# A hybrid decoder block: a shrinking lead of first products in the up-projection, and the weight sums of the down-projection spread over three stages

## The chip, the cores and the metric

The kernel runs on one core of one Trainium2 chip. The metric is the device time of one execution in microseconds (us). TensorE is called PE, VectorE DVE, ScalarE ACT, GpSimd POOL, and SyncE, which issues the transfers, SP.

## The reference, cut to what matters

One layer of a decoder block for 1024 tokens of width 1024, in float32. Two token mixers are projected, gated and merged, and a gated MLP follows:

```
y_a = o_a @ w_nsa_branch;  y_b = o_r @ w_ret_branch
x = x + (gate_a * y_a + gate_b * y_b) @ w_mix_out
h = rms_norm(x, norm_ffn_w)
u = causal_dwconv(h @ w_ffn_up, ffn_conv_w, ffn_conv_b)      # 1024 -> 2 x 2816, width 3
u_gate, u_val = split(u, 2)
x = x + (silu(u_gate) * u_val) @ w_ffn_down                  # 2816 -> 1024
return rms_norm(x, norm_final_w)
```

## The kernel before, in words

Each float32 operand of a product is held as a high and a low part, and a product is three passes on PE: high by high, low by high, high by low (`mm3`, line 283). A split is two instructions: ACT writes the high part `wh` (line 175, `split`), and DVE or POOL subtracts it from the source to get the low part `wl` (line 176).

**Up** is done by 2x2 blocks in Winograd's form, with seven products in place of eight. A step `f` (of 22) makes one tile of 128 gate and one of 128 value columns, 7 products of 12 matmuls (128x512) each, 84 in all. Two of them, "11" and "21", need no sums: `start_up` multiplies a11 by block B11, copies the bank to SBUF (ACT, `p1`), and a12 by B21 is added to the same bank. Five need sums: s2·t2, s3·t3, s1·t1, then a22·t4 and s4·B22, where t1 to t4 are sums of h's blocks (made once, split by `sums`) and s1 to s4 are sums of the step's weights, made by DVE a step ahead (`other_weights`, lines 1214 to 1220). a22·t4 is added to the bank `q` of s3·t3, so its first matmul has to wait until DVE has read that bank for `u3` (line 1244). The step's end is DVE's `cg[:, 1]` (line 1255); then follow the convolution, silu and multiplication (lines 1230 to 1259), and the store of the result, `act`.

The raw weights come as 512 KB tiles by `raw_up`: `v` (the pair a21, a22) and `g` (a11, a12), through the two buffers of `wraw`. SP issues in its program order, and a transfer into a buffer waits for the last reader of the tile that was there. Before `up`'s first step, `LEAD` = 5 pairs of the products "11" and "21" are computed ahead, in the place that is called the lead here; h's last transposed blocks (`piece`) and their sums stand between them.

For down, the sums of its weights (11 groups, `t_sums`: four loads, four DVE instructions, four stores of 256 KB each) are made earlier and stored: six in the branch-a stage (the product with w_nsa_branch, line 1012, which also holds transposes), five in the mix stage (the product with w_mix_out). The w_ret_branch stage stands between the two.

The order on each engine is mostly made by a scheduler from the order of emission, which acts as priority, with waits on semaphores. PE's order in the lead and in the mix stage's second half is the order of the code (`manual_schedule`).

Of the kernel before, what the change touches and what calls it, by code (L numbers as in the profile page):

```python
# [10 lines left out]
F32 = mybir.dt.float32  # L11
# [7 lines left out]
P = 128  # L19
# [144 lines left out]
def hybrid_block(ctx: ExitStack, tc: tile.TileContext, a, c, out):  # L164
# [839 lines left out]
    for ch in range(2):  # L1004
        nx = Weights(w_a, 0, 4, [(512, 512)]) if ch == 0 else Weights(w_b, 0, KT, [(0, 512)])
        for i in range(4):
            m = gated(ch * 4 + i)
            ps = ps2.tile([P, S], F32, name="mm2")
            for half in range(2):
                mm3(ps[:, half * 512:half * 512 + 512], lambda part, kt: gw.at(part, kt, i * P, P),  # L1010
                    lambda part, kt: oaT[part][kt][:, half * 4:half * 4 + 4, :].rearrange("p t q -> p (t q)"), 4)
            nc.vector.tensor_mul(m, ps, m)
            ma.append(m)
            if len(t_left) > 5:
                x, y = ([q[:, 0:512], q[:, 512:S]] for q in
                        (mp.tile([P, S], F32, name="tq", tag="gb", bufs=3) for _ in range(2)))
                t_sums(t_left.pop(0), x, y)
            transposed_split(ps1, o_r[ch * 4 + i], *orT, ch * 4 + i)
        gw = nx
    with ort:  # L1020
        craw = wraw.tile([P, 2, 512], F32, name="wr").rearrange("p a b -> p (a b)")
        for i in range(4):
            src = a["ffn_conv_b"][0] if i == 3 else a["ffn_conv_w"][0, i]
            nc.sync.dma_start(craw[:2 * FT, i * P:(i + 1) * P], src.rearrange("(f p) -> f p", p=P))
        pc = ps1.tile([P, 4, P], F32, name="tp")
        for i in range(4):
            nc.tensor.transpose(pc[:, i, :2 * FT], craw[:2 * FT, i * P:(i + 1) * P], ident[:2 * FT, :2 * FT])
        nc.vector.tensor_copy(cw, pc[:, :, :2 * FT])
        for ch in range(2):
            nx = Weights(w_b, 0, KT, [(512, 512)]) if ch == 0 else Weights(w_mix, 0, KT, [(0, 512)])  # L1030
            for i in range(4):
                j = ch * 4 + i
                m = gated(KT + j)
                ps = ps2.tile([P, S], F32, name="mm2")
                mm3t(ps, gw, i * P, orT, KT)
                nc.vector.tensor_mul(m, ps, m)
                nc.vector.tensor_add(m, m, ma[j])
                mhj = big2.tile([P, S], F32R, name="mh", tag="big2")
                mlj = big.tile([P, S], F32R, name="ml", tag="big")
                split(mhj, mlj, m)  # L1040
                mh.append(mhj)
                ml.append(mlj)
            gw = nx
    ms.close()
    pss_.close()
# [32 lines left out]
    def piece(t, h):  # L1078

        at = slice((t % 4) * P, (t % 4) * P + P)  # L1080
        got = []
        for kh in range(2):
            pt = psX.tile([P, 4, P], F32, name="f")
            for i in range(4):
                nc.tensor.transpose(pt[:, i, :], h[kh][:, i * P:(i + 1) * P], ident)
            full = mx.tile([P, 4, P], F32, name="pc", bufs=16)
            nc.scalar.activation(full, pt, AF.Copy)
            if t < 4 or kh:
                k = ("21" if kh else "11") if t < 4 else "22"
                nc.scalar.activation(bh[k][:, :, at], pt, AF.Copy)  # L1090
                nc.vector.tensor_tensor(bl[k][:, :, at], pt, f32(bh[k][:, :, at]), OP.subtract)
            got.append(full)
        low[t] = got
        if t < 4:
            return
        (b11, b21), (b12, b22) = low[t - 4], low[t]
        side = nc.vector if t == NT - 1 else nc.gpsimd
        nc.vector.tensor_tensor(b11, b12, b11, OP.subtract)
        side.tensor_tensor(b12, b22, b12, OP.subtract)
        nc.vector.tensor_tensor(b22, b22, b11, OP.subtract)  # L1100
        side.tensor_tensor(b21, b21, b22, OP.subtract)

    waiting = []

# [16 lines left out]
    pair = []  # L1121
    for t in range(NT):
        residual(t, 0)
        if t in (1, 3, 5, 6, 7) and len(t_left):
            four = [mx.tile([P, 512], F32, name="tq", tag="pc", bufs=16) for _ in range(4)]
            t_sums(t_left.pop(0), four[:2], four[2:])
        if not pair:
            pair = [bank() for _ in range(2 if t in (0, NT - 2) else 1)]
            for k in range(0, KT, 2):
                for i, ps in enumerate(pair):  # L1130
                    mo(ps, t + i, k, k + 2)
        ps = pair.pop(0)
        nc.vector.tensor_add(x1[t][0], ps, x1[t][0])
# [38 lines left out]
    def first_weights(f):  # L1172

        g = raw_up(f, 0)
        p = parts2(g, nc.gpsimd)
        return {k: [x[:, i] for x in p] for i, k in enumerate(("a11", "a12"))}, g

    def prod(ps, w, k, first=True, last=True):
        mm3(ps, lambda part, kt: w[part][:, kt * P:(kt + 1) * P], lambda part, kt: (bh, bl)[part][k][:, kt, :], 4,
# [2 lines left out]
    def start_up(w):  # L1182
        x = bank()
        prod(x, w["a11"], "11")
        p1 = c2()
        nc.scalar.activation(p1, x, AF.Copy)  # L1186
        return x, p1

    sums([4, 5])
    uw, begun = {}, {}  # L1190
    for f in range(LEAD):
        uw[f], _ = first_weights(f)
        begun[f] = start_up(uw[f])
        if f in (0, 2):
            t = waiting[0][0]
            piece(*waiting.pop(0))
            sums([t])
        prod(begun[f][0], uw[f]["a12"], "21", False, True)
    pe_order.close()
    mix.close()  # L1200

# [5 lines left out]

    act_d = [dram.tile([P, 2, 512], F32, name=f"act{f}") for f in range(FT)]

    def other_weights(f, w, g=None):  # L1210
        v = raw_up(f, 1)
        g = g or raw_up(f, 0)
        s = c4()
        nc.vector.tensor_add(s[:, 0], v[:, 0], v[:, 1])
        nc.vector.tensor_sub(s[:, 1], s[:, 0], g[:, 0])
# [16 lines left out]
        nc.vector.scalar_tensor_tensor(y[:, 2:], src[:, :S - 2], cw[:, 0, f:f + 1], y[:, 2:], op0=OP.mult, op1=OP.add)  # L1232
        return y

    def up(f, w, begun=None):
        x, p1 = begun or start_up(w)
        y = bank()
        prod(y, w["s2"], "t2")
        u2 = c2()
# [4 lines left out]
        nc.vector.tensor_add(u3, q, u2)  # L1244
        z = bank()
        prod(z, w["s1"], "t1")
        cg, cv = c4(), c4()
        nc.vector.tensor_add(cv[:, 1], z, u3)
        if not begun:
            prod(x, w["a12"], "21", False, True)  # L1250
        nc.scalar.activation(cg[:, 0], x, AF.Copy)
        prod(q, w["a22"], "t4", False, True)
        nc.vector.tensor_add(cv[:, 0], q, u2)
        prod(z, w["s4"], "22", False, True)
# [5 lines left out]
        yg = yg.rearrange("p (a b) -> p a b", b=512)  # L1260
        nc.sync.dma_start(act_d[f], yg)

    def weights(f):
        if f in uw:
            return other_weights(f, uw.pop(f))
        return other_weights(f, *first_weights(f))

    nx = weights(0)
    for f in range(FT):
        w, nx = nx, weights(f + 1) if f + 1 < FT else None  # L1270
        up(f, w, begun.pop(f, None))
    tp.close()
    ups.close()


    STEPS = [(j, min(2, HT - j)) for j in range(0, HT, 2)]
    NS = len(STEPS)
    keep = ctx.enter_context(tc.tile_pool(name="keep", bufs=1, side="right", reuse_waits="tile"))
    sparts = ctx.enter_context(tc.tile_pool(name="sparts", bufs=3, side="right", reuse_waits="tile"))
    raws = ctx.enter_context(tc.tile_pool(name="raws", bufs=3, side="right", reuse_waits="tile"))  # L1280
    xp = ctx.enter_context(tc.tile_pool(name="xp", bufs=1, reuse_waits="tile"))
    kp2 = ctx.enter_context(tc.tile_pool(name="keep2", bufs=1, reuse_waits="tile"))
    W = {"b11": (0, 0), "b21": (1, 0), "b22": (1, 1)}
    A = {"a11": (0, 0), "a12": (1, 0), "a21": (0, 1), "a22": (1, 1)}
    kept = {}

    def fetch_a(k, i, dst):
        (kh, sh), (j, n) = A[k], STEPS[i]
        for x in range(n):
            nc.sync.dma_start(dst[:, x], act_d[kh * HT + j + x][:, sh])  # L1290
        return dst

    def held(k, i):
        if (k, i) not in kept:
# [29 lines left out]
            "a22": lambda i: held("a22", i)}  # L1324

    def prepared(sk, tk, i):
        j, n = STEPS[i]
        t = wraw.tile([P, 2, 512], F32, name="wr")
        if tk in W:
            kh, nh = W[tk]  # L1330
            r0 = (kh * HT + j) * P
            src = w_dn[r0:r0 + n * P, nh * 512:nh * 512 + 512].rearrange("(k p) n -> p k n", p=P)
        else:
            src = t_d[int(tk[1]) - 1][j:j + n].rearrange("k p n -> p k n")
        nc.sync.dma_start(t[:, :n], src)
        s = S_OF[sk](i)
        got = []
        for x, pool, names in ((s, sparts, ("sh", "sl")), (t, wpool, ("wh", "wl"))):
            p = [pool.tile([P, 2, 512], F32R, name=k) for k in names]
            split(p[0][:, :n], p[1][:, :n], x[:, :n])  # L1340
            got.append(p)
        return got
# [68 lines left out]
                ("s3", "t3", "y", True, done_7, True), ("s4", "b22", "z", True, done_3, True),  # L1411
                ("a22", "t4", "y", True, done_4, False)]
    units = [(i, j) for i in range(7) for j in range(NS)]
    ready = {}
    banks = {}
    later = []
    AHEAD = 2
# [1 line left out]
    for at, (i, j) in enumerate(units):  # L1419
        for x in units[at:at + AHEAD + 1]:  # L1420
            if x not in ready:
                ready[x] = prepared(*PRODUCTS[x[0]][:2], x[1])
        if i == 1:
            held("a21", j)
            held("a22", j)
        if i == 1 and j:
# [61 lines left out]
```

## Time and profile before

| | |
|---|---|
| median of 3 runs (lowest, highest) | 1812.72 us (1809.72, 1813.13) |
| profiled execution, its own time | 1812.5 us |
| its span | 1810.7 us |
| PE busy | 97% of the span |
| mean granted clock of PE | 0.99 |
| stretch from the end of step 0 to up's end | 1184.87 to 1585.24 us |

The median is over whole executions; the span is the part of the profiled one that the trace covers, and times in the trace count from its start. A granted clock of 1.00 is PE at 2.4 GHz.

### The profile page before, as it was taken

The numbers are of one execution on the slowest core, as the hardware profiler recorded it, in microseconds if no ns is written. First come the engines' busy times: TensorE is split into PE (matmuls) and PEld (weight loads), VectorE is DVE, ScalarE is ACT, GpSimd is POOL, SyncE is SP. The second block draws the span as 40 slices with busy tenths as digits, with TensorE's granted clock in tenths as the row PEclk, the third lists the DMA queues.
The fourth block names the chain that finished last, engine by engine and source line by source line (L and its number), as shares of the span: only waits on it lengthen the run. The fifth ranks groups of instructions, "written<-read, shape, count | busy, mean of one in ns | idle before, by whom it ended". The sixth has DMA issues, their size and how long they took to land.

```text
span 1810.7 us, 22500 instructions
## 1 busy us (share of the span) xinstructions
PE 1750.6 (97%) x8331; PEld 1434.6 (79%) x8331; DVE 1186.5 (66%) x2337; ACT 804.2 (44%) x1464; POOL 126.6 (7%) x78
## 2 busy tenths in 40 slices
PE   7999999999999999999989999789999999999998
PEld 6987888888788888888868877667888888878886
DVE  7445877777875554455644446767767777678666
ACT  6334666666662344136332215434444444343344
POOL 0000020110100000000000002301121211000000
PEclk9999999999999999999989999899999999999999
DMA  6121010110202111101682383322322322395353
GB/s 227 55 82 53 19 56 32 36 59 18 71 24 94 47 37 57 47 1 47 231 270 93 93 300 137 99 70 70 104 71 82 93 70 87 108 354 189 94 163 111
DMA packets 87418, 178.88 MB, mean 99 GB/s; under 512 B 8508, under 2 KB 18316, under 8 KB 87308
## 3 DMA queue, kind: packets, MB, share of 16 engines
q1 hardware_dynamic: 87308, 177.44, 30.2%
q8 instruction: 65, 1.06, 0.2%
q14 instruction: 45, 0.37, 0.1%
HBM read 137.57 MB, written 39.85 MB: 98 GB/s over the span
## 4 chain that ended last, share of the span: by engine, by line
PE 60%; DVE 5%; DMA 4%; ACT 2%; issue 2%; SPq 1%; POOL 1%; DVEq 0%; POOLq 0%; ACTq 0%
PE f L283 33%; PE mm L283 19%; PE fill L772 2%; DMA tq<-in_w_ffn_down 2%; PE po L826 1%; PE pv L718 1%; PE pt L706 1%; PE sc L610 1%; DMA wr<-in_w_ffn_up 1%; PE pst L826 1%; DMA wr<-in_w_mix_out 0%; ACT wh L209 0%; PE pss L871 0%; DVE c L1231 0%; DVE c L1232 0%
## 5 line engine op out<-in xcount | busy, mean ns | idle before, releaser
L283 PE MATMUL mm<-wh,hh 128*128 128x512 f32 (+1 forms) x576 | 224.0, 389 | 0.5 <-ACT hh L175 0.5
L283 PE MATMUL mm<-wh,hl 128*128 128x512 f32 (+1 forms) x576 | 219.8, 382 | 0.0
L283 PE MATMUL mm<-wl,hh 128*128 128x512 f32 (+1 forms) x576 | 219.8, 382 | 0.0
L209 ACT ACTIVATE wh<-wr 128x1024 fp32r<-128x1024 f32 (+1 forms) x72 | 74.6, 1037 | 167.0 <-PE mm L283 83.2
L713 DVE TENSOR_TENSOR pl<-pt,ph 128x512 fp32r<-128x512 f32 (+1 forms) x148 | 100.6, 686 | 41.8 <-ACT ph L710 41.2
L283 PEld LDWEIGHTS mm<-wh,hl 128*128 128x128 f32 x576 | 108.8, 189 | 20.6 <-DVE hl L176 0.3
L283 PEld LDWEIGHTS mm<-wh,hh 128*128 128x128 f32 x576 | 108.8, 189 | 20.2 <-ACT hh L175 0.9
L283 PE MATMUL f<-wh,sh 128*128 128x512 f32 x308 | 121.6, 395 | 3.3 <-ACT sh L175 3.3
L710 ACT ACTIVATE ph<-pt 128x512 fp32r<-128x512 f32 (+1 forms) x148 | 87.7, 594 | 82.8 <-PE pt L706 74.5
L283 PEld LDWEIGHTS mm<-wl,hh 128*128 128x128 f32 x576 | 108.9, 189 | 19.5 <-DVE wl L215 0.5
L283 PE MATMUL f<-wl,sh 128*128 128x512 f32 x308 | 121.5, 395 | 0.0
L283 PE MATMUL f<-wh,sl 128*128 128x512 f32 x308 | 120.7, 395 | 0.0
L283 PE MATMUL f<-bh,wh 128*128 128x512 f32 x264 | 105.0, 398 | 11.9 <-ACT c L1186 11.9
L176 POOL TENSOR_TENSOR wl<-wr,wh 128x1024 fp32r<-128x1024 f32 x22 | 53.6, 2438 | 898.3 <-ACT wh L175 883.4
L283 PE MATMUL f<-bht,wh 128*128 128x512 f32 x264 | 104.8, 397 | 8.3 <-ACT wh L175 8.3
L772 PE MATMUL fill<-hh,wh 128*128 128x512 f32 x256 | 104.5, 408 | 3.0 <-ACT sg L784 2.0
L283 PE MATMUL f<-bht,wl 128*128 128x512 f32 x264 | 105.0, 398 | 2.2 <-DVE wl L176 2.2
L628 ACT ACTIVATE big<-big,st 128x640 f32<-128x640 f32 (+7 forms) x128 | 93.4, 730 | 28.1 <-DVE st L624 27.3
L215 DVE TENSOR_TENSOR wl<-wr,wh 128x1024 fp32r<-128x1024 f32 (+1 forms) x60 | 71.5, 1193 | 51.2 <-ACT wh L209 50.2
L283 PE MATMUL f<-blt,wh 128*128 128x512 f32 x264 | 104.4, 395 | 0.0
L283 PE MATMUL f<-bl,wh 128*128 128x512 f32 x264 | 104.1, 394 | 0.0
L283 PE MATMUL f<-bh,wl 128*128 128x512 f32 x264 | 103.4, 393 | 0.0
(282 smaller groups left out, 4127.6 us busy)
## 6 DMA issues: line engine op xcount, KB each, us to landing
wr<-in_w_ffn_up SPq DMA_DIRECT2D x49, 512.0 KB, 4.7
wr<-in_w_in SPq DMA_DIRECT2D x40, 512.0 KB, 3.7
tq<-in_w_ffn_down SPq DMA_DIRECT2D x44, 256.0 KB, 4.7
t<-tq SPq DMA_DIRECT2D x44, 256.0 KB, 3.0
act<-c SPq DMA_DIRECT2D x22, 512.0 KB, 2.8
wr<-t SPq DMA_DIRECT2D x20, 512.0 KB, 3.5
a<-act SPq DMA_DIRECT2D x33, 256.0 KB, 6.0
gate<-sg SPq DMA_DIRECT2D x32, 256.0 KB, 2.0
```

Of the source, the lines that this page charges most:

```text
L176: (engine or nc.vector).tensor_tensor(lo, src, f32(hi), OP.subtract)
L209: nc.scalar.activation(hi[:, :, :self.n], self.raw[len(self.hi)], AF.Copy)
L215: self.engine.tensor_tensor(lo[:, :, :self.n], self.raw[j], f32(self.hi[j][:, :, :self.n]), OP.subtract)
L283: nc.tensor.matmul(ps, stat(sp, kt), mov(mp, kt), start=(first and n == 0), stop=(last and n == 3 * nk - 1), skip_group_check=more)
L610: nc.tensor.matmul(out[:, c0:c0 + n], q[:, h, :], mov, start=(q is box["h"]), stop=(q is box["l"]))
L628: nc.scalar.activation(probs[b][h], probs[b][h], AF.Exp, scale=-1.0, bias=stat["nm", b][:, h:h + 1], accum_out=stat["w", b][:, h:h + 1])
L706: nc.tensor.transpose(bx["pt"][:rows, h, :], probs[h][:, k * P:k * P + rows], ident)
L710: nc.scalar.activation(bx["h"][:rows], bx["pt"][:rows], AF.Copy)
L713: nc.vector.tensor_tensor(bx["l"][:rows], bx["pt"][:rows], f32(bx["h"][:rows]), OP.subtract)
L718: nc.tensor.matmul(acc["pv"], v, bx[part][:rows].rearrange("p h q -> p (h q)"), start=start, stop=stop)
L772: nc.tensor.matmul(fx["ps"], w.at(sp, kt, i * P, P), hT[mp][:, kt, half * 512:half * 512 + 512], start=(n == 0), stop=(n == 3 * KT - 1))
L826: nc.tensor.matmul(ps[:, h, :], stat[sp][:, h, :], mov[mp][:, h, :], start=(first and n == 0), stop=(last and n == 2))
```

## The change

In `up`, each step first starts the pairs of later steps: the lead is 5 pairs at the start and shrinks to one (`max(1, LEAD - f // 4)` ahead). Their products "11" and "21" are emitted before a22·t4 of the current step. The weights of the pairs are now fetched apart from those of the sums: three raw tiles in a step where before there were two (from step 5 on, `g` was fetched once for both uses). `sums` is emitted after the five leads instead of between them. `piece` makes all its four sums on DVE. The 11 groups of `t_sums` are spread 4, 3 and 4 over the branch-a stage, the w_ret_branch stage and the mix stage. The last step of up also prepares the first unit of down. PE's work is the same in number and kind.

```diff
-            if len(t_left) > 5:
+            if (ch * 4 + i) % 2 == 0:
                 x, y = ([q[:, 0:512], q[:, 512:S]] for q in
                         (mp.tile([P, S], F32, name="tq", tag="gb", bufs=3) for _ in range(2)))
                 t_sums(t_left.pop(0), x, y)
...
+                if j in (2, 4, 6):
+                    x, y = ([q[:, 0:512], q[:, 512:S]] for q in
+                            (mp.tile([P, S], F32, name="tq", tag=f"ma{j - k}") for k in (2, 1)))
+                    t_sums(t_left.pop(0), x, y)
...
-        side = nc.vector if t == NT - 1 else nc.gpsimd
         nc.vector.tensor_tensor(b11, b12, b11, OP.subtract)
-        side.tensor_tensor(b12, b22, b12, OP.subtract)
+        nc.vector.tensor_tensor(b12, b22, b12, OP.subtract)
         nc.vector.tensor_tensor(b22, b22, b11, OP.subtract)
-        side.tensor_tensor(b21, b21, b22, OP.subtract)
+        nc.vector.tensor_tensor(b21, b21, b22, OP.subtract)
...
-        if t in (1, 3, 5, 6, 7) and len(t_left):
+        if t % 2 and t_left:
...
-    sums([4, 5])
-    uw, begun = {}, {}
+    fw, begun = {}, {}
     for f in range(LEAD):
-        uw[f], _ = first_weights(f)
-        begun[f] = start_up(uw[f])
+        fw[f] = first_weights(f)
+        begun[f] = start_up(fw[f])
         if f in (0, 2):
-            t = waiting[0][0]
             piece(*waiting.pop(0))
-            sums([t])
-        prod(begun[f][0], uw[f]["a12"], "21", False, True)
+        prod(begun[f][0], fw[f]["a12"], "21", False, True)
+    sums([4, 5, 6])
+    sums([7])
...
-    def other_weights(f, w, g=None):
-        v = raw_up(f, 1)
-        g = g or raw_up(f, 0)
+    def other_weights(f):
+        w = {}
+        v, g = raw_up(f, 1), raw_up(f, 0)
...
-    def up(f, w, begun=None):
-        x, p1 = begun or start_up(w)
+    def up(f, w, x, p1, ahead):
+
+        cg, cv = c4(), c4()
+        nc.scalar.activation(cg[:, 0], x, AF.Copy)
         y = bank()
         prod(y, w["s2"], "t2")
...
-        if not begun:
-            prod(x, w["a12"], "21", False, True)
-        nc.scalar.activation(cg[:, 0], x, AF.Copy)
+        for k in ahead:
+            begun[k] = start_up(fw[k])
+            prod(begun[k][0], fw.pop(k)["a12"], "21", False, True)
         prod(q, w["a22"], "t4", False, True)
...
+    at = LEAD
     for f in range(FT):
-        w, nx = nx, weights(f + 1) if f + 1 < FT else None
-        up(f, w, begun.pop(f, None))
+        w, nx = nx, other_weights(f + 1) if f + 1 < FT else None
+        upto = min(FT, f + 1 + max(1, LEAD - f // 4))
+        for k in range(at, upto):
+            fw[k] = first_weights(k)
+        if f == FT - 1:
+            s = fetch_a("a11", 0, wraw.tile([P, 2, 512], F32, name="wr"))
+            ready[0, 0] = [parts2(s, nc.vector), parts2(fetch_t("b11", 0), nc.vector)]
+        up(f, w, *begun.pop(f), range(at, upto))
+        at = max(at, upto)
```

What this makes of the order on the engines is seen at three places.

PE, in the middle of up, where a22·t4 begins. `bh11` and `bl11` are the parts of B11, the names with t1 and t4 those of the sums; `a22h`, `a22l`, `wh` and `wl` are weights. Before, step 8:

```order
L283 MATMUL f_11800<-bh11_9529,wl_11640 128x512 [waits Pool_49]
L283 MATMUL f_11800<-bh11_9529,wh_11639 128x512
L283 MATMUL f_11800<-bl11_9532,wh_11639 128x512
L283 MATMUL f_11800<-bh11_9529,wl_11640 128x512
L283 MATMUL f_11800<-bh11_9529,wh_11639 128x512
L283 MATMUL f_11800<-bl11_9532,wh_11639 128x512
L283 MATMUL f_11800<-bh11_9529,wl_11640 128x512
L283 MATMUL f_11693<-bht4_10404,a22h_11522 128x512 [waits DVE_49]
L283 MATMUL f_11693<-blt4_10405,a22h_11522 128x512
```

Now, step 2:

```order
L283 MATMUL f_11029<-bht1_10400,wl_10837 128x512
L283 MATMUL f_11014<-bht4_10402,a22h_10847 128x512 [waits DVE_49]
L283 MATMUL f_11014<-blt4_10403,a22h_10847 128x512
L283 MATMUL f_11014<-bht4_10402,a22l_10848 128x512
L283 MATMUL f_11014<-bht4_10402,a22h_10847 128x512
L283 MATMUL f_11014<-blt4_10403,a22h_10847 128x512
L283 MATMUL f_11043<-bh11_9543,wh_10992 128x512 [waits Activation_49]
L283 MATMUL f_11043<-bl11_9546,wh_10992 128x512
L283 MATMUL f_11043<-bh11_9543,wl_10993 128x512 [waits Pool_49]
```

Before, the product with B11 of a later step stood ahead of a22·t4, after t2, t3, t1 and the step's own product "21". Now a22·t4 follows t1 directly: five matmuls, then B11 of a pair of the lead (12 matmuls), four of a22·t4, B21 of the pair (12), three of a22·t4, and s4·B22 (12). Steps 3, 6, 7, 10, 11, 14, 15, 18, 19 and 20 read the same, and steps 5, 9, 13 and 17 nearly so (a22·t4 cut into 6, 2 and 4). Step 1 has B11 ahead of a22·t4. Steps 4, 8, 12, 16 and 21 start no pair; there a22·t4 and B22 follow t1 (and 11 matmuls of the next step's t2).

SP, the raw weights of a step and the store of a result. Before:

```order
L1169 DMA wr_11010<-in_w_ffn_up 128x1024 [waits DMAHW7_49,DVE_49,Pool_49]
L1169 DMA wr_11012<-in_w_ffn_up 128x1024 [waits DMAHW0_49,DVE_49]
L1261 DMA act2_10650<-c4_10999 128x1024 [waits DVE_49]
```

Now; `wr_10990` becomes the `wh_10992` and `wl_10993` of the rows on PE, and `wr_11107` and `wr_11109` are v and g of the sums of a later step:

```order
L1172 DMA wr_10990<-in_w_ffn_up 128x1024 [waits DMAHW1_49,DVE_49,Pool_49]
L1172 DMA wr_11107<-in_w_ffn_up 128x1024 [waits DMAHW3_49,DVE_49]
L1172 DMA wr_11109<-in_w_ffn_up 128x1024 [waits DMAHW5_49,Pool_49]
L1264 DMA act2_10648<-c4_11096 128x1024 [waits DVE_49]
```

There are three tiles in place of two through the same two buffers. The first takes the buffer of a v, whose last reader on DVE is line 1221 (1219 before), the second that of a g, the third that of the first, which POOL's split has read.

SP, in the branch-a stage, around the load of the fifth gate tile (`ma<-gate_1647`). Before:

```order
L202 DMA wr<-in_w_ret_branch 128x2x512
L989 DMA tq<-in_w_ffn_down 128x512
L990 DMA tq<-in_w_ffn_down 128x512
L202 DMA wr<-in_w_ret_branch 128x2x512
L978 DMA ma_8796<-gate_1647 128x1024
L997 DMA t_8525<-tq 128x512
```

Now:

```order
L997 DMA t_8526<-tq 128x512
L202 DMA wr<-in_w_ret_branch 128x2x512
L978 DMA ma_8768<-gate_1647 128x1024
L202 DMA wr<-in_w_ret_branch 128x2x512
L989 DMA tq<-in_w_ffn_down 128x512
L990 DMA tq<-in_w_ffn_down 128x512
```

In the whole queue, 16 loads of down's weights and 13 stores of sums stood ahead of this gate tile before, and 8 loads and 8 stores now.

## Rows read from the trace of the kernel before

**Rows 1.** The page: share of busy time, and the granted clock in 40 slices.

```profile
PE 1750.6 (97%) x8331; PEld 1434.6 (79%) x8331; DVE 1186.5 (66%) x2337; ACT 804.2 (44%) x1464; POOL 126.6 (7%) x78
PEclk9999999999999999999989999899999999999999
```

**Rows 2.** Windows: stretch, length, busy us of each engine, PE's clock, DMA share, GB/s.

```profile
860.00:934.00 74.00, 66.57 (x307) 53.48 (x305) 46.03 (x59) 26.03 (x34) 0.00 (x0) 0.95 0.75 252
934.00:1022.00 88.00, 87.57 (x364) 70.43 (x365) 34.92 (x32) 23.01 (x22) 0.00 (x0) 0.94 0.30 101
1132.00:1140.00 8.00, 3.71 (x9) 2.96 (x10) 7.88 (x17) 5.87 (x12) 1.28 (x1) 0.57 0.23 80
1166.00:1237.00 71.00, 59.39 (x240) 45.56 (x239) 49.67 (x58) 24.81 (x27) 5.16 (x4) 0.96 0.26 88
1237.00:1585.00 348.00, 348.00 (x1506) 282.71 (x1504) 252.47 (x288) 148.76 (x161) 62.07 (x34) 1.00 0.27 86
```

**Rows 3.** Timeline of PE: first matmuls after its waits (start, length, and idle time before).

```profile
934.43 0.82 PE L283 MATMUL mm<-orT,wh 128*128 128x512 f32 x2 [2.61 <-DVE ma L1012]
1078.68 0.49 PE L283 MATMUL f<-wh,mh 128*128 128x512 f32 x1 [2.15 <-ACT wh L209]
1136.29 0.80 PE L283 MATMUL f<-bh,wh 128*128 128x512 f32 x1 [7.04 <-ACT c L1186]
1146.69 0.80 PE L283 MATMUL f<-bh,wh 128*128 128x512 f32 x1 [3.07 <-ACT c L1186]
1213.25 0.50 PE L283 MATMUL f<-bht,wh 128*128 128x512 f32 x1 [3.59 <-ACT wh L175]
1588.50 0.50 PE L283 MATMUL f<-wh,sh 128*128 128x512 f32 x1 [3.26 <-ACT sh L175]
```

**Rows 4.** Timeline of SP in steady up: three stores of results, and weight fetches.

```profile
1382.22 0.33 SPq L1261 DMA_DIRECT2D act<-c  x1
1401.15 0.33 SPq L1261 DMA_DIRECT2D act<-c  x1
1401.79 2.03 SPq L1169 DMA_DIRECT2D wr<-in_w_ffn_up  x2
1420.07 0.33 SPq L1261 DMA_DIRECT2D act<-c  x1
```

**Rows 5.** Timeline of DVE, PE, ACT and POOL in one step of steady up.

```profile
1392.45 0.69 DVE L1255 TENSOR_TENSOR c<-f,c 128x512 f32<-128x512 f32 x1 [2.04 <-PE f L283]
1401.04 0.69 DVE L1219 TENSOR_TENSOR c<-wr 128x512 f32<-128x512 f32 x1
1404.17 0.69 DVE L1244 TENSOR_TENSOR c<-f,c 128x512 f32<-128x512 f32 x1
1405.65 0.40 PE L283 MATMUL f<-bht,a22h 128*128 128x512 f32 x1
1406.83 1.06 ACT L175 ACTIVATE wh<-wr 128x1024 fp32r<-128x1024 f32 x1 [0.84 <-DMA wr<-in_w_ffn_up]
1407.97 2.41 POOL L176 TENSOR_TENSOR wl<-wr,wh 128x1024 fp32r<-128x1024 f32 x1 [15.61 <-ACT wh L175]
```

**Rows 6.** The page's transfers: line, count, size, median us from issue to landing.

```profile
wr<-in_w_ffn_up SPq DMA_DIRECT2D x49, 512.0 KB, 4.7
```

**Rows 7.** Timeline of PE: the last of the 24 matmuls after each lead wait.

```profile
1143.23 0.39 PE L283 MATMUL f<-bh,wl 128*128 128x512 f32 x1
1153.51 0.40 PE L283 MATMUL f<-bh,wl 128*128 128x512 f32 x1
```

**Rows 8.** Timeline in the lead: a sum on DVE alone, and beside POOL.

```profile
1127.48 0.68 DVE L1098 TENSOR_TENSOR pc<-pc 128x512 f32<-128x512 f32 x1
1138.72 2.40 POOL L176 TENSOR_TENSOR wl<-wr,wh 128x1024 fp32r<-128x1024 f32 x1 [7.07 <-ACT wh L175]
1138.92 2.74 DVE L1098 TENSOR_TENSOR pc<-pc 128x512 f32<-128x512 f32 x1
```

**Rows 9.** Timeline of DVE: the end of step 0.

```profile
1184.87 0.69 DVE L1255 TENSOR_TENSOR c<-f,c 128x512 f32<-128x512 f32 x1 [2.04 <-PE f L283]
```

More of the change, by code (lines that the diff above doesn't have):

```diff
@@ L1175, in first_weights @@
         p = parts2(g, nc.gpsimd)
-        return {k: [x[:, i] for x in p] for i, k in enumerate(("a11", "a12"))}, g
+        return {k: [x[:, i] for x in p] for i, k in enumerate(("a11", "a12"))}
     def prod(ps, w, k, first=True, last=True):
@@ L1246, in up @@
         prod(z, w["s1"], "t1")
-        cg, cv = c4(), c4()
         nc.vector.tensor_add(cv[:, 1], z, u3)
-        if not begun:
-            prod(x, w["a12"], "21", False, True)
-        nc.scalar.activation(cg[:, 0], x, AF.Copy)
+        for k in ahead:
+            begun[k] = start_up(fw[k])
+            prod(begun[k][0], fw.pop(k)["a12"], "21", False, True)
         prod(q, w["a22"], "t4", False, True)
@@ L1261, in up, with fetch_a, fetch_t @@
         nc.sync.dma_start(act_d[f], yg)
[L1263 to L1268, printed above, removed]
-    for f in range(FT):
-        w, nx = nx, weights(f + 1) if f + 1 < FT else None
-        up(f, w, begun.pop(f, None))
+    STEPS = [(j, min(2, HT - j)) for j in range(0, HT, 2)]
+    NS = len(STEPS)
+    A = {"a11": (0, 0), "a12": (1, 0), "a21": (0, 1), "a22": (1, 1)}
+    W = {"b11": (0, 0), "b21": (1, 0), "b22": (1, 1)}
+    def fetch_a(k, i, dst):
+        (kh, sh), (j, n) = A[k], STEPS[i]
+        for x in range(n):
+            nc.sync.dma_start(dst[:, x], act_d[kh * HT + j + x][:, sh])
+        return dst
+    def fetch_t(k, i):
+        j, n = STEPS[i]
+        t = wraw.tile([P, 2, 512], F32, name="wr")
+        if k in W:
+            kh, nh = W[k]
+            r0 = (kh * HT + j) * P
+            src = w_dn[r0:r0 + n * P, nh * 512:nh * 512 + 512].rearrange("(k p) n -> p k n", p=P)
+        else:
+            src = t_d[int(k[1]) - 1][j:j + n].rearrange("k p n -> p k n")
+        nc.sync.dma_start(t[:, :n], src)
+        return t
+    ready = {}
+    nx = other_weights(0)
+    at = LEAD
+    for f in range(FT):
+        w, nx = nx, other_weights(f + 1) if f + 1 < FT else None
[7 more added lines that the diff above has]
+        at = max(at, upto)
     tp.close()
     ups.close()
-    STEPS = [(j, min(2, HT - j)) for j in range(0, HT, 2)]
-    NS = len(STEPS)
     keep = ctx.enter_context(tc.tile_pool(name="keep", bufs=1, side="right", reuse_waits="tile"))
@@ L1282, in hybrid_block @@
     kp2 = ctx.enter_context(tc.tile_pool(name="keep2", bufs=1, reuse_waits="tile"))
-    W = {"b11": (0, 0), "b21": (1, 0), "b22": (1, 1)}
-    A = {"a11": (0, 0), "a12": (1, 0), "a21": (0, 1), "a22": (1, 1)}
     kept = {}
[L1287 to L1291, printed above, removed]
     def held(k, i):
@@ L1326, in prepared @@
     def prepared(sk, tk, i):
[L1327 to L1335, printed above, removed]
+        n = STEPS[i][1]
+        t = fetch_t(tk, i)
         s = S_OF[sk](i)
@@ L1413, in hybrid_block @@
     units = [(i, j) for i in range(7) for j in range(NS)]
-    ready = {}
     banks = {}
@@ L1423, in hybrid_block @@
         if i == 1:
+            held("a11", j)
             held("a21", j)
```

## The prediction

> **What bounds the kernel now.** I read the page's shares first: PE is busy 97% of the span at nearly full clock everywhere [rows 1]. So time can be won only from PE's waits and the stretches of low clock, and lost wherever PE has to wait anew. The windows then show where that is [rows 2]. In steady up, from 1237 to 1585, PE is busy 348.00 of 348.00 us at clock 1.00: nothing is to be won there. The branch-a stage (860 to 934) leaves 74.00 - 66.57 = 7.4 us idle, and up's early steps (1166 to 1237) 71.00 - 59.39 = 11.6 us. The timeline of PE names the waits [rows 3]: on DVE's gate product, line 1012; in the mix stage on a weight's high part; two in the lead on ACT's copy of a bank; in the early steps on the high parts of s1 to s4; and 3.26 us where down begins.
>
> The last view is one step of steady up, engine by engine. Stores of results follow each other by 1401.15 - 1382.22 = 18.93 us [rows 4], and 84 matmuls fill that, so one costs 18.93 / 84 = 0.2253 us. I count from R, the start of DVE's `cg[:, 1]` at 1392.45 [rows 5]. From there DVE goes in its own order through the convolution of the step just ended and the next weights' sums: line 1219 ends at 1401.73 (R + 9.3), and `u3` (line 1244) at 1404.86 (R + 12.4). a22·t4 may overwrite its bank only after `u3`. It began at 1405.65, R + 13.2: PE had 58 other matmuls (13.1 us) to do until then, so DVE's order cost nothing. That margin of 0.8 us is what the prediction hangs on.
>
> **The change in up.** DVE's order within a step stays as it was; PE's does not. From step 2 on, between R and a22·t4 there are now only t2, t3 and t1: 36 x 0.2253 = 8.1 us. PE is through with them at R + 8.1 and has to wait for `u3` until R + 12.4. PE does its matmuls in the order shown, so B11 of the pair, which needs no `u3`, stands behind that wait.
>
> Then comes a second wait. Five matmuls on (R + 13.5), B11 of the pair needs its weights' high part from ACT, and its third matmul the low part from POOL. Their raw tile is the first of SP's three fetches, and waits for the buffer that line 1221 frees, the former 1219: R + 9.3. Before, the same fetch went out at 1401.79, R + 9.3, ACT began its split at 1406.83, 5.04 us later, and POOL's part ran from 1407.97 for 2.41 us, to R + 17.9 [rows 4, 5]; the page's median from issue to landing, 4.7, agrees [rows 6]. Before, these parts were needed only in the next step. Now the third matmul of B11 cannot go before R + 17.9, and behind it stand 10 + 4 + 12 + 3 + 12 = 41 matmuls, 9.24 us. The step takes 27.2 us where it took 18.93.
>
> On top comes the clock. It was 0.57 between 1132 and 1140 [rows 2], where PE had waited 7.04 us [rows 3]. The 24 matmuls that followed took 1143.23 - 1136.29 = 6.94 us from the first's start to the last's; after the wait of 3.07 us, 1153.51 - 1146.69 = 6.82 us [rows 3, 7]. At 0.2253 it would be 23 x 0.2253 = 5.18. So a wait of 3 to 7 us cost 1.64 to 1.76 us more. The new step has two waits, of 4.3 and 4.4 us with 1.1 us of matmuls between. The bounds are no loss and one for each, 3.4. I take one, 1.7, since the two waits lie as close as one: T = 28.9 us.
>
> Steps that start no pair have no second wait: R + 12.4, then 24 matmuls, 17.8 us. From the end of step 0 to up's end there are 16 steps with a pair (1 to 3, 5 to 7, 9 to 11, 13 to 15, 17 to 20) and 5 without. Sum: 16 x 28.9 + 5 x 17.8 = 551.4 us, where before it took 1585.24 - 1184.87 = 400.4 [rows 3, 9]: **+151.0**. (3.26 of idle time end at 1588.50; up ends at 1585.24.) Step 0 has 24 matmuls more, **+5.4**. The lower bound of T is a fetch that costs nothing: 12.4 + 48 x 0.2253 = 23.2. The upper is 27.2 + 3.4 = 30.6.
>
> The Trainium skill, "PSUM — Partial Sum Buffer", section "Engine vs sequencer instructions", says that matmuls start and complete in program order. By it the pair cannot fill the wait for `u3`, which speaks against this change; if matmuls could pass each other, the steps would stay near 18.93 us. No row of before shows a matmul passing another or failing to.
>
> The 17 more fetches of 512 KB cost nothing by themselves: transfers have a share of 0.27 in up [rows 2]. The copy of x at the step's head lies in ACT's idle time (148.76 of 348 us busy).
>
> **The change elsewhere.** *Branch-a*: 16 loads and 13 stores stood ahead of the fifth gate tile, now 8 and 8. What can be won is the idle time of 7.4 us, the clock's 0.05 x 74 = 3.7, and what follows into the next stage, 0.06 x 88 + 0.4 = 5.7: 16.8 in all; the other bound is nothing. I take **-14**: the stage's transfers (share 0.75) were what came late, and only its first waits stay. *The w_ret_branch stage* receives 3 groups: 12 DVE instructions of some 0.7 us, 8 us beside 53 idle ones, and transfers beside a share of 0.30: nothing. Without that cover they would cost up to the 8 us. *Mix* keeps 4 of 5 groups: **-1**, between 0 and the 2.15 of the wait. *Lead*: six POOL subtractions go to DVE, and the sums' splits go behind the banks' copies on ACT. A subtraction took 0.68 us alone and 2.74 us beside POOL's split [rows 8]; that split stays. Of the waits of 7.04 + 3.07 I take a third, **-3.3**, between 0 and all 10.1. *Into down*: the first unit is prepared a step ahead, **-3.3**, the whole wait; nothing is the other bound.
>
> The Trainium skill, "SBUF — State Buffer", section "SBUF: two separate sides", has DVE's instructions with two SBUF inputs and GpSimd's lock each other out for a whole instruction; the row of 2.74 us agrees. By it alone the whole 10.1 us would not go, since POOL's splits remain.
>
> **Sum.** Against the profiled execution's 1812.5 us, which is 0.2 below the median: 1812.5 + 151.0 + 5.4 - 14 - 1 - 3.3 - 3.3 = **1947 us**.
>
> **The rivals.** *The fetch does not bind*: buffers come free earlier than I read, and only `u3` is waited for, T = 23.2: 16 x 23.2 + 89.0 - 400.4 = +59.8, so 1856 us. For it: the fetches run ahead through the early steps. Against: the buffer's last reader is line 1221 in every step, and SP's row waits for it. 0.14.
>
> *More half clock*, T = 30.6: +178.2, so 1974 us. For it: two waits in a step, every step. Against: much of the low clock may fall into the waits, as part of 1132 to 1140 did. 0.11.
>
> *Faster*: the lead really fills PE, because DVE reaches `u3` by R + 8.1 and the pair's weights are there. DVE would have to do its 12.4 us of work in 8.1, or a pair's tile land a step early. Then every step is bound by PE's 84 matmuls, and the early waits go too: 11.6 us and 0.04 x 71 = 2.8 of clock. 1812.5 - 21.6 - 14.4 = 1776 us. DVE is busy 252 of 348 us, so it has idle time, but that lies after `u3`, where it waits for PE (2.04 us before R). It decides whether `u3` ends before R + 8.1. 0.06.
>
> *The gains cancel the waits*, about 1812 us: this needs T near 20.5, below the bound. 0.02.
>
> **How the numbers follow.** My forecast, T from 27.2 to 30 with the gains as above, has 0.67; at T = 27.2 it gives 1920 us. The range from 1855 to 1980 takes in the first two rivals. 0.2% (3.6 us) is what a measurement of this kernel can tell from no change. Slower holds my forecast and two rivals, 0.92; faster 0.06; same 0.02.
>
> **What the profile would show.** The stores of results come some 29 us apart in steps with a pair and 18 without, clock below 1.00 all through up, and PE's first a22·t4 matmul waits some 4 us for DVE line 1248, B11's first for ACT's `wh`, its third for POOL's `wl`. DVE's chain from R to `u3` still takes 12.4 us. The branch-a stage and the way into down have lost their waits. I am wrong if PE has no wait ahead of a22·t4, or if `wl` of the pair is done before R + 13.

## The result and the profile after

The changed kernel takes 1950.67 us (median; 1946.73 to 1955.19) beside 1812.93 us before: a ratio of 1.0763, 95% interval 1.0736 to 1.0791. The forecast was 1947 us. The profiled execution's span is 1952.7 us, 142.0 more than before.

The page: share of busy time, the granted clock in 40 slices, and three of the costliest groups with their idle time and what ended it.

```profile
PE 1804.7 (92%) x8331; PEld 1458.6 (75%) x8331; DVE 1190.9 (61%) x2343; ACT 805.7 (41%) x1464; POOL 118.9 (6%) x72
PEclk9999999999999999999999998897888888799999
...
L283 PE MATMUL f<-bh,wh 128*128 128x512 f32 x264 | 119.4, 452 | 25.3 <-ACT wh L175 18.6
...
L283 PE MATMUL f<-bh,wl 128*128 128x512 f32 x264 | 117.7, 446 | 19.1 <-POOL wl L176 19.1
...
L283 PE MATMUL f<-bht,a22h 128*128 128x512 f32 x88 | 44.1, 501 | 68.6 <-DVE c L1248 68.6
```

PE's share falls from 97 to 92% [rows 1], and the slices of up have a lower clock. The three groups are the three waits that the prediction named: a22·t4 on `u3` (now line 1248) 68.6 us, B11 of the pair on ACT's high part 18.6 and on POOL's low part 19.1.

Windows of the new kernel (columns as in [rows 2]): the branch-a stage, most of up, and one step of up, from R to the first a22·t4, on to B11's third matmul, and to the next R.

```profile
855.00:923.00 68.00, 67.97 (x324) 55.96 (x323) 38.87 (x49) 25.52 (x33) 0.00 (x0) 1.00 0.64 216
...
1216.00:1719.00 503.00, 401.50 (x1473) 302.04 (x1474) 259.82 (x297) 150.15 (x161) 58.48 (x33) 0.85 0.24 76
...
1417.72:1430.18 12.46, 8.36 (x37) 6.39 (x35) 11.58 (x14) 6.04 (x6) 0.00 (x0) 0.96 0.23 69
1430.18:1435.42 5.24, 3.72 (x7) 1.99 (x7) 1.68 (x2) 1.06 (x1) 2.35 (x1) 0.50 0.37 138
1435.42:1446.94 11.52, 11.52 (x42) 9.26 (x43) 0.69 (x1) 1.23 (x2) 1.28 (x1) 0.83 0.14 47
```

The same step in the timeline of all engines.

```profile
1417.72 0.69 DVE L1258 TENSOR_TENSOR c<-f,c 128x512 f32<-128x512 f32 x1 [4.77 <-PE f L283]
1426.31 0.68 DVE L1221 TENSOR_TENSOR c<-wr 128x512 f32<-128x512 f32 x1
1427.06 8.66 SPq L1172 DMA_DIRECT2D wr<-in_w_ffn_up  x3
1429.43 0.69 DVE L1248 TENSOR_TENSOR c<-f,c 128x512 f32<-128x512 f32 x1
1430.18 0.80 PE L283 MATMUL f<-bht,a22h 128*128 128x512 f32 x1 [4.10 <-DVE c L1248]
1431.88 1.06 ACT L175 ACTIVATE wh<-wr 128x1024 fp32r<-128x1024 f32 x1 [1.99 <-DMA wr<-in_w_ffn_up]
1432.99 0.79 PE L283 MATMUL f<-bh,wh 128*128 128x512 f32 x1 [0.31 <-ACT wh L175]
1433.02 2.35 POOL L176 TENSOR_TENSOR wl<-wr,wh 128x1024 fp32r<-128x1024 f32 x1 [19.07 <-ACT wh L175]
1435.42 0.79 PE L283 MATMUL f<-bh,wl 128*128 128x512 f32 x1 [1.21 <-POOL wl L176]
1446.94 0.69 DVE L1258 TENSOR_TENSOR c<-f,c 128x512 f32<-128x512 f32 x1 [2.05 <-PE f L283]
```

R is 1417.72. Line 1221 frees the buffer at R + 9.3, the fetch goes out at once, ACT's split begins 4.82 us after it, POOL's low part ends at R + 17.65; `u3` ends at R + 12.4. PE waits 4.10, 0.31 and 1.21 us, and between the first and the third wait it does its matmuls at a clock of 0.50. The step takes 29.22 us.

A step that starts no pair is called pairless here. In the step behind it 11 of the matmuls with t2 are already done, so PE reaches a22·t4 sooner and waits longer, as where R is 1387.24.

```profile
1398.91 0.79 PE L283 MATMUL f<-bht,a22h 128*128 128x512 f32 x1 [5.88 <-DVE c L1248]
```

By stages, as differences of the two spans: branch-a and what follows up to the mix stage -13.5; mix +4.3; lead -6.2; step 0 +4.9; from the end of step 0 to up's end 558.1 in place of 400.4, +157.7; the way into down -3.4; down -1.8. Sum +142.0.

### The profile page after: what moved, and what is told of

Its sections match the earlier page's. It is cut to its first block, busy times and chain, and to the rows that moved or that the text cites. A ratio compares the mean times of both kernels' runs of the same rounds, so it can differ in the third digit from the quotient of the medians.

```text
span 1952.7 us, 22576 instructions
## 1 busy us (share of the span) xinstructions
PE 1804.7 (92%) x8331; PEld 1458.6 (75%) x8331; DVE 1190.9 (61%) x2343; ACT 805.7 (41%) x1464; POOL 118.9 (6%) x72
## 3 DMA queue, kind: packets, MB, share of 16 engines
q1 hardware_dynamic: 90044, 186.88, 29.3%
## 4 chain that ended last, share of the span: by engine, by line
PE 49%; DVE 10%; DMA 8%; ACT 3%; issue 3%; POOL 2%; SPq 1%; POOLq 0%; ACTq 0%; DVEq 0%
PE f L283 24%; PE mm L283 18%; DMA wr<-in_w_ffn_up 5%; DVE c L1233 3%; DVE c L1234 2%; PE fill L772 2%; DMA tq<-in_w_ffn_down 2%; POOL wl L176 2%; ACT c L1232 1%; DVE c L1262 1%; PE po L826 1%; PE pv L718 1%; ACT wh L175 1%; PE pt L706 1%; PE sc L610 1%
## 5 line engine op out<-in xcount | busy, mean ns | idle before, releaser
L283 PE MATMUL f<-bh,wh 128*128 128x512 f32 x264 | 119.4, 452 | 25.3 <-ACT wh L175 18.6
L1256 DVE TENSOR_TENSOR c<-f,c 128x512 f32<-128x512 f32 x22 | 15.2, 692 | 200.4 <-PE f L283 200.4
L283 PE MATMUL f<-bh,wl 128*128 128x512 f32 x264 | 117.7, 446 | 19.1 <-POOL wl L176 19.1
L713 DVE TENSOR_TENSOR pl<-pt,ph 128x512 fp32r<-128x512 f32 (+1 forms) x148 | 100.6, 687 | 41.9 <-ACT ph L710 41.3
L283 PEld LDWEIGHTS mm<-wh,hl 128*128 128x128 f32 x576 | 108.6, 189 | 20.4 <-DVE hl L176 0.3
L283 PEld LDWEIGHTS mm<-wl,hh 128*128 128x128 f32 x576 | 108.8, 189 | 19.5 <-DVE wl L215 0.5
L283 PE MATMUL f<-bl,wh 128*128 128x512 f32 x264 | 116.1, 440 | 0.0
L283 PE MATMUL f<-bht,a22h 128*128 128x512 f32 x88 | 44.1, 501 | 68.6 <-DVE c L1248 68.6
```

The source lines that it names most:

```text
L283: nc.tensor.matmul(ps, stat(sp, kt), mov(mp, kt), start=(first and n == 0), stop=(last and n == 3 * nk - 1), skip_group_check=more)
L713: nc.vector.tensor_tensor(bx["l"][:rows], bx["pt"][:rows], f32(bx["h"][:rows]), OP.subtract)
```

## The experiments

"R" and "pair" are used as in the prediction. A diff is against the changed kernel, unless another is named. Each ratio is to the kernel before.

**The pairs at the step's end.**

```diff
-        for k in ahead:
-            begun[k] = start_up(fw[k])
-            prod(begun[k][0], fw.pop(k)["a12"], "21", False, True)
         prod(q, w["a22"], "t4", False, True)
         nc.vector.tensor_add(cv[:, 0], q, u2)
         prod(z, w["s4"], "22", False, True)
         nc.vector.tensor_add(cg[:, 1], z, u2)
+        for k in ahead:
+            begun[k] = start_up(fw[k])
+            prod(begun[k][0], fw.pop(k)["a12"], "21", False, True)
```

> The pairs of the lead are emitted at the step's end, after s4·B22, in place of before a22·t4; PE's order has B11 and B21 of the pair between B22 and the next step's t2, t3 and t1, 60 matmuls (13.5 us) between R and a22·t4. Fetches stay three to a step. If PE's order made the two waits: steps with a pair ahead of them near 18.9 us, the steps behind a pairless one 17.8 to 20, so from the end of step 0 to up's end some 395 us in place of 558, and 1788 us in all (1778 to 1800). If the third fetch through two buffers is itself what bounds a step, the steps stay near 29 us and the time near 1950.

Measured: 1809.57 us, ratio 0.999 (0.9977 to 1.0004). From the end of step 0 to up's end it took 421.5 us. A window over more than three steps, and one of PE's waits in the timeline:

```profile
1262.00:1333.00 71.00, 71.00 (x304) 57.09 (x303) 49.39 (x56) 28.01 (x31) 12.26 (x7) 0.99 0.29 90
```

```profile
1259.69 0.50 PE L283 MATMUL f<-bht,a22h 128*128 128x512 f32 x1 [4.10 <-DVE c L1248]
```

Steps with a pair ahead of them take 19.5 us with PE busy throughout, those behind a pairless one 19.9, with the wait of 4.10 us. So PE's order made the waits, and three fetches through two buffers do not bound a step. The total missed its expectation by 22 us, for reasons of counting: this order puts step 0's pair behind the end of step 0 (5.5 us), 84 matmuls take 19.4 us and not 18.9 (see below), four waits of 4.10 remain with their low clock, and steps 1 and 21 wait 2.3 and 3.3 us, step 1 for the pair's parts and step 21 for its bank's copy.

**A buffer for the pair's raw tile.** `cp` goes from 8 buffers to 7.

```diff
+    def own_up(f):
+        r = cpool.tile([P, 2, 512], F32, name="wg", bufs=1)
...
-        g = raw_up(f, 0)
+        g = raw_up(f, 0) if f < LEAD else own_up(f)
```

> The pair's raw tile gets a buffer of its own (one c4 buffer less, 7, pays for it), so that it lands a step early; PE's order is that of the changed kernel but for one a22·t4 matmul ahead of B11 in place of five. Only the wait on the fetch goes, that for u3 stays. My theory: a step with a pair takes 12.4 + 48 x 0.2253 = 23.2 us, with the low clock of one wait 24.9, so 16 x 4.4 = 70 us less than the changed kernel: 1880 (1850 to 1895). If only u3 mattered, no change: 1950. If only the fetch mattered, steps of 18.9 and 1785.

Measured: 1936.65 us, ratio 1.0681 (1.0657 to 1.0704): 14 under the changed kernel in place of 70. Timeline of a step whose R is 1381.26 (behind a pairless one):

```profile
1392.31 1.06 ACT L175 ACTIVATE wh<-c 128x1024 fp32r<-128x1024 f32 x1 [1.93 <-DVE c L1227]
1392.93 0.80 PE L283 MATMUL f<-bht,a22h 128*128 128x512 f32 x1 [5.88 <-DVE c L1253]
1393.27 1.04 ACT L175 ACTIVATE wh<-wg 128x1024 fp32r<-128x1024 f32 x1
1394.39 2.62 POOL L176 TENSOR_TENSOR wl<-wg,wh 128x1024 fp32r<-128x1024 f32 x1 [14.06 <-ACT wh L175]
1397.06 0.80 PE L283 MATMUL f<-bh,wl 128*128 128x512 f32 x1 [1.48 <-POOL wl L176]
```

The tile was there, but ACT takes its split in its own order, behind that of s3 and s4, which waits for DVE until R + 11. POOL is done at R + 15.8 where it was R + 17.7, so PE waits again, 1.48 us. The fetch alone was not the second wait: without the buffer's wait the split's place in ACT's order holds the weights back nearly as long. My expectation failed there.

**The pair's weights a step earlier.**

```diff
+        then = min(FT, f + 2 + max(1, LEAD - (f + 1) // 4))
-        for k in range(at, upto):
-            fw[k] = first_weights(k)
+        for k in range(at, max(upto, then)):
+            if k not in fw:
+                fw[k] = first_weights(k)
```

> The pair's weights are fetched and split a step earlier, through the same two buffers. PE then has t2, t3, t1, B11 and three matmuls of the next t2 (51, or 48 where three of t2 were done before) between R and a22·t4: 10.8 to 11.5 us, where u3 comes at 12.4. My theory: waits of 1 to 1.6 us in a step, 12.4 + 36 x 0.2253 = 20.5 us a step, 5 steps of 17.8 to 18.4: 1807 (1795 to 1830). If the third fetch binds by itself: near 1950.

Measured: 1822.59 us, ratio 1.0052 (1.0035 to 1.0068). From step 5 on, steps with a pair take 20.2 to 20.5 us. With both parts in time the scheduler puts B11 ahead of a22·t4. The wait that is left is one of 0.83 us in most steps, and it is another than I expected: on DVE's low part of the next step's s2, ahead of its product with t2, not on `u3`.

```profile
1285.61 1.22 DVE L176 TENSOR_TENSOR wl<-c,wh 128x1024 fp32r<-128x1024 f32 x1
1286.88 0.51 PE L283 MATMUL f<-bht,wl 128*128 128x512 f32 x1 [0.83 <-DVE wl L176]
```

**The earlier parts alone, up as before.** The kernel before with `t_sums` spread 4, 3, 4, the pieces' sums on DVE, and `sums` behind the five leads.

> The kernel before with the change's earlier parts alone: sums of down's weights 4, 3 and 4, the pieces' sums on DVE, the sums' splits after the five leads; up as before. From the changed kernel's trace: branch-a 13.5 us less, mix 4.3 more, lead 6.2 less, so 1797 (1791 to 1803). If up's early steps take back what comes sooner, because their weights are late, 1803 to 1810.

Measured: 1796.46 us, ratio 0.9904 (0.9878 to 0.9929). The early parts gain as expected, and up gives back little: from the end of step 0 to up's end it takes 401.7 us where it took 400.4.

**The late weights alone.** PE's order in up is that of the code.

```diff
+    up_order = ExitStack()
+    up_order.enter_context(tc.manual_schedule(engines={PE}))
     for f in range(FT):
...
+    up_order.close()
```

> The changed kernel with PE's order in up written out as the code has it: t2, t3, t1, then B11 and B21 of the pair, a22·t4, B22. The wait for u3 is gone (60 matmuls lie ahead of a22·t4), the pair's late weights stay. If the two waits lie over each other in time, the late weights alone cost what both did: low part at R + 17.7, then 46 matmuls of 0.2308, 10.6, some 0.7 for the bank's copy between B11 and B21, and 1.7 of low clock: 30.7 us a step, 1970 in all (1940 to 1990). If each wait cost its own share, a step falls by the 4.1 of u3 to 25.2 and the time to 1885.

Measured: 2002.21 us, ratio 1.1052 (1.103 to 1.1074). PE's waits in one step:

```profile
1449.25 0.79 PE L283 MATMUL f<-bh,wh 128*128 128x512 f32 x1 [7.02 <-ACT wh L175]
1451.68 0.80 PE L283 MATMUL f<-bh,wl 128*128 128x512 f32 x1 [1.21 <-POOL wl L176]
1456.25 0.50 PE L283 MATMUL f<-bh,wh 128*128 128x512 f32 x1 [0.69 <-ACT c L1189]
```

**The wait for `u3` alone.** The pair's tile has its own buffer as above, its split is emitted ahead of `other_weights`, and PE's order is written out with a22·t4 ahead of the pair.

```diff
-        for k in ahead:
...
         prod(q, w["a22"], "t4", False, True)
         nc.vector.tensor_add(cv[:, 0], q, u2)
+        for k in ahead:
```

> PE's order in up written out as t2, t3, t1, a22·t4, B11, B21, B22; the pair's raw tile has a buffer of its own (one c4 buffer less) and its split is emitted ahead of the sums of the next step's weights, so that both parts are there a step early. Only the wait for u3 is left, and some 0.7 for the bank's copy between B11 and B21: 12.5 + 48 x 0.2308 + 0.7 = 24.3 us a step, 26.0 with the low clock of one wait, 27.7 with that of two: 16 x 3.3 = 53 us under the changed kernel, 1898 (1870 to 1925). If the fetch was all that cost, steps near 19.4 and 1790.

Measured: 1926.19 us, ratio 1.0624 (1.0607 to 1.0642).

```profile
1442.14 0.80 PE L283 MATMUL f<-bht,a22h 128*128 128x512 f32 x1 [4.10 <-DVE c L1253]
1451.17 0.50 PE L283 MATMUL f<-bh,wh 128*128 128x512 f32 x1 [0.69 <-ACT c L1194]
```

Both runs came out above their ranges, by 12 and 1 us, since the low clock cost more than I gave it, also in the pairless steps, where PE still waits 4.10 us for `u3` in either run (20.4 to 21.2 us a step, where I had 17.8). Over the 16 steps with a pair the late weights alone make a step of 31.8 us in the mean (30.6 to 34.2), the wait for `u3` alone one of 27.2, where 84 matmuls need 19.4. Alone they cost 12.4 and 7.8 us, each with the 0.69 us for the bank's copy between B11 and B21, which this order adds. Together, in the changed kernel, they cost 10.6: 29.3 us a step, for 81.25 matmuls (18.75 us) in the mean, since the four steps behind a pairless one hold 73. From the end of step 0 to up's end the late weights alone take 606.5 us, `u3` alone 534.0, both 558.1. They lie over each other: taking away the wait for `u3` alone, by writing out PE's order, made the kernel slower. The order offers a reason that no run takes apart: five matmuls of a22·t4, which stood ahead of the late weights, now stand behind them.

**The convolution later.** The changed kernel, with the end of a step emitted after `u3` of the next.

```diff
+    tail = []
...
         nc.vector.tensor_add(u3, q, u2)
+        if tail:
+            tail.pop(0)()
         z = bank()
...
-        yg = conv(cg.rearrange("p a b -> p (a b)"), f)
+        tail.append(lambda: finish(f, cg, cv))
+
+    def finish(f, cg, cv):
+        yg = conv(cg.rearrange("p a b -> p (a b)"), f)
...
+    tail.pop(0)()
```

> The changed kernel with the convolution, silu and product of a step emitted after u3 of the next step. DVE then makes u2 and u3 between the convolution's instructions, and the scheduler puts B11 of the pair ahead of a22·t4, its weights fetched at the end of the step before. If DVE's order from R to u3 and the late weights are the whole loss, PE does its 1668 matmuls from the end of step 0 on at 0.2308 with hardly a wait: 385 to 393 us in place of 558, and 1782 us in all (1775 to 1795), under the kernel before by 17 to 37. If DVE then becomes the bound, or the stores of results come too late for the buffers, steps of 20 and more and 1800 to 1830.

Measured: 1778.96 us, ratio 0.9817 (0.9802 to 0.9832), faster than both kernels. Windows over up, and the timeline of a step whose R is 1284.55:

```profile
1174.00:1554.00 380.00, 380.00 (x1643) 306.94 (x1642) 312.86 (x329) 162.78 (x178) 67.03 (x35) 1.00 0.32 110
```

```profile
1284.55 0.69 DVE L1262 TENSOR_TENSOR c<-f,c 128x512 f32<-128x512 f32 x1 [1.61 <-PE f L283]
1285.46 2.42 POOL L176 TENSOR_TENSOR wl<-wr,wh 128x1024 fp32r<-128x1024 f32 x1 [1.82 <-ACT wh L175]
1291.87 0.68 DVE L1250 TENSOR_TENSOR c<-f,c 128x512 f32<-128x512 f32 x1
1295.47 0.40 PE L283 MATMUL f<-bht,a22h 128*128 128x512 f32 x1
1303.99 0.69 DVE L1262 TENSOR_TENSOR c<-f,c 128x512 f32<-128x512 f32 x1 [1.85 <-PE f L283]
```

`u3` is done at R + 8.0, the pair's low part at R + 3.3; a22·t4 waits for nothing, and a step of 84 matmuls takes 19.4 us. The scheduler has put B11 of the pair ahead of a22·t4 here too, which begins only at R + 10.9. PE is busy 380.00 of 380.00 us at clock 1.00.

**The same with sums of down's weights spread 5, 3 and 3.** The conditions become `ch * 4 + i in (0, 1, 2, 4, 6)` and `t in (1, 3, 5)`.

> As the run before, and the groups of sums of down's weights are spread 5, 3 and 3 in place of 4, 3 and 4. In the changed kernel the fourth group of the mix stage stood ahead of the split of w_mix_out's last tile on DVE, and the mix stage took 4.3 us more than before. If that is the reason, 3 to 5 us under the run before; if the branch-a stage gives them back (its transfers have a share of 0.64), no difference or 1 to 3 us more.

Measured: 1778.44 us, ratio 0.9812 (0.9795 to 0.9829), no difference. The waits in the mix stage fall from 2.35 and 0.76 us to 0.34 and the stage from 99.7 us to 95.4, but the branch-a stage waits 3.12 and 1.70 us again, and the mix stage begins 7.4 us later.

**Which edit shortened the lead.** The run with the earlier parts alone, the pieces' sums on POOL again.

```diff
+        side = nc.vector if t == NT - 1 else nc.gpsimd
         nc.vector.tensor_tensor(b11, b12, b11, OP.subtract)
-        nc.vector.tensor_tensor(b12, b22, b12, OP.subtract)
+        side.tensor_tensor(b12, b22, b12, OP.subtract)
         nc.vector.tensor_tensor(b22, b22, b11, OP.subtract)
-        nc.vector.tensor_tensor(b21, b21, b22, OP.subtract)
+        side.tensor_tensor(b21, b21, b22, OP.subtract)
```

> The kernel of the run with the earlier parts alone and up as before (1796.5), with four of the pieces' sums on POOL again in six places, as before the change. It tells which of the two edits made the lead 6.2 us shorter. If it was the subtractions on DVE, 1801 to 1804; if it was that the sums' splits stand behind the five leads, 1796 to 1798; my theory, half each, 1799.

Measured: 1797.66 us, ratio 0.9917 (0.9887 to 0.9946); the interval overlaps that of the run with the sums on DVE, so the totals do not tell the two apart. In the profiles the lead takes 36.5 us with the sums on POOL, 35.1 on DVE, 41.3 before: of the 6.2 us, 4.8 come with the splits' place behind the five leads.

**What the shrinking lead is worth.** The earlier parts alone, up as before, and the convolution later.

> The run with the earlier parts alone and up as before, with the convolution of a step emitted after u3 of the next step, as in the run of 1779. It tells what the shrinking lead itself is worth once the waits are gone. There the five leads are used up in steps 0 to 4, which have 60 matmuls (13.9 us) each; if DVE's work bounds such a step at 15.8 us (what a pairless step took in the run of 1779), five such steps in a row lose 5 x 2 us: 1789 (1784 to 1795). If the lead's shape is worth nothing, 1779.

Measured: 1785.43 us, ratio 0.9847 (0.9818 to 0.9877). The early steps lose less than I expected: steps 1 to 4 take 12.9 to 16.2 us, and PE waits 2.4 us in all. From its first matmul with t2 to the end of its last step, up takes 405.6 us here and 405.7 with the shrinking lead. So once the waits are gone the lead's shape is worth nothing that these profiles show. Of the 6.5 us between the two medians 3.5 are the wait into down, which only the change removes; the rest is within what can be told, as the two intervals (0.9818 to 0.9877 and 0.9802 to 0.9832) overlap.

## Why the prediction was right

**The mechanism** was right: DVE's chain from R to `u3` still takes 12.4 us, PE waits 4.10 us for it (forecast 4.3; 5.88 behind a pairless step), the pair's low part is done at R + 17.2 to 18.9 (17.9), and all other waits of PE from the end of step 0 to up's end are 5.5 of 111.8 us. In the run with the convolution later both dependences are met in time, and all waits and all low clock in up are gone, so up held no third cause of any size. That run comes to the time of the rival "faster" (1779 us for 1776), but not by its path alone: `u3` is done at R + 8.0, as the rival asked, yet with B11 ahead of a22·t4 it is needed only at R + 10.9. No run shows that R + 8.1 was necessary. One sign was wrong: the clock was below 1.00 only in steps with a pair, and 1.00 in the pairless ones.

**T**, forecast 28.9, is 29.3 on average over the 16 steps (26.4 to 30.6), and the pairless steps 18.4 (17.8), the last 15.3. That T came so near is partly luck: three sizes behind it were off, and the errors cancelled. A matmul costs 0.2308 us, not 0.2253: in the stretch of [rows 4] a step held 82 matmuls, because B11's place moved by two in every step, and I divided by 84; in the runs here a step of 84 without waits takes 19.4. With the 81.25 matmuls that a step held in the mean this makes 18.75 us for 18.93. PE's waits in a pair's step add up to 6.6 us, where the forecast held 8.3 (4.3 and 4.4, less two matmuls in the second), since matmuls at low clock filled part of the time in which the weights were late; and the low clock cost 29.3 - 18.75 - 6.6 = 3.9 us, not 1.7. In that the rival "more half clock" was the nearer: 3.9 is more than its 3.4, and only the shorter waits kept T below its 30.6.

**That the two waits could be added** was a way to count T and not a property of each: alone they cost 7.8 and 12.4, together 10.6. The rival "the fetch does not bind", T = 23.2, was priced without the low clock: with `u3` as the only long wait a step takes 27.2. And the second wait was not the buffer alone, as I had it, but also ACT's order.

**The terms elsewhere**: branch-a -13.5 (forecast -14), step 0 +4.9 (+5.4), into down -3.4 (-3.3). The lead, -6.2, was undersized at -3.3: I ascribed it to POOL's subtractions and the splits alike, and it is mostly the splits. The mix stage had the wrong sign, +4.3 for -1: w_mix_out's last tile is fetched once DVE has done the low part of an earlier tile, and that stands behind a group's sums. PE waits 3.67 and 0.77 us, and the clock falls to 0.93 behind it (1066 to 1116).

```profile
1056.59 0.69 DVE L993 TENSOR_TENSOR tq<-tq 128x512 f32<-128x512 f32 x1 [1.15 <-DMA tq<-in_w_ffn_down]
1058.66 2.35 DVE L215 TENSOR_TENSOR wl<-wr,wh 128x1024 fp32r<-128x1024 f32 x2
1059.90 0.38 SPq L202 DMA_DIRECT2D wr<-in_w_mix_out  x1
1066.68 0.50 PE L283 MATMUL f<-wh,mh 128*128 128x512 f32 x1 [3.67 <-ACT wh L209]
```

The run with three groups there bears this out: its waits are 0.34 us. Runs with the same code there as the changed kernel gave 98.7 to 102 us for that stage, before 97.7, so about half of the +4.3 is no steady cost. The errors cancel here too: mix and lead together came to -1.9 for a forecast of -4.3, and down's -1.8, of which 1.4 are six matmuls done within up, had no term.

## What to carry to other kernels

Work that is emitted ahead to fill a wait helps only if it stands ahead of the waiting instruction in the engine's order and its operands are there by then: read both from the built order and from the timeline. In these runs the scheduler put it behind where its operands came late (after step 1 of the changed kernel) and ahead where they came in time. When an in-order engine meets two waits, price them together; taking one away may save nothing. If an engine's chain decides a wait, move what that chain does not need (here the convolution) behind it before adding work elsewhere.

## What the runs showed of the hardware

A wait of 4.10 us in front of PE cost more than itself whenever it came back in each step: with that wait and one of 0.69 a step of 84 matmuls took 27.2 us, so 27.2 - 19.4 - 4.8 = 3.0 us went to the clock, where I had 1.7 from the waits of the lead. With the pairs at the step's end, where the wait came in one step of four, such a step of 60 matmuls (60 x 0.2308 = 13.85 us) took 19.87 us: 19.87 - 13.85 - 4.10 = 1.9 us for the clock. In the changed kernel the clock was 0.50 (1.2 GHz) right after the wait and 0.83 in the rest of the step, and 0.85 in the mean over up.
